# Start offsets of the split weight tiles, and the number of bias buffers, in a two-layer encoder

## The chip, the cores and the metric

The kernel runs on one core of one Trainium2 chip. The core has a matrix engine (TensorE, PE in the rows), which multiplies a stationary operand (the weights, loaded by a separate instruction, PEld) with a moving operand streamed past it; three engines for elementwise work (VectorE or DVE, ScalarE or ACT, GpSimd or POOL); and SyncE (SP), which here only issues DMA transfers, in its own order. [...] The metric is the device time of one execution in microseconds (us).

## The reference, cut to what matters

A trunk of two layers over 256 tokens of width 1024, all in fp32. Each layer is a SwiGLU feed-forward of width 2816, three attention mixers that share one input projection, their gated sum with an output projection, and a second feed-forward.

```python
def swiglu(h, w_in, w_out):
    g, u = jnp.split(h @ w_in, 2, axis=-1)
    return (jax.nn.silu(g) * u) @ w_out

for l in range(DEPTH):                                   # DEPTH = 2
    x = x + 0.5 * swiglu(rmsnorm(x, norm_ffn1[l]), w_ffn1_in[l], w_ffn1_out[l])
    h = rmsnorm(x, norm_mix[l])
    qa, ka, va, qb_, kb, vb, qc, kc, vc, gate_logits = jnp.split(h @ w_in[l], split_points, axis=-1)
    y_a = mixer_a(...)        # dense attention with rotary, 8 heads
    y_b = mixer_b(...)        # windowed attention, 8 heads, with a relative bias
    y_c = mixer_c(...)        # differential attention, 4 heads x 2 maps, with a relative bias
    branches = jnp.einsum('bsnw,nwd->bsnd', jnp.stack([y_a, y_b, y_c], axis=2), w_branch[l])
    merged = jnp.sum(jax.nn.sigmoid(gates) * branches, axis=2)
    x = x + merged @ w_out[l]
    x = x + 0.5 * swiglu(rmsnorm(x, norm_ffn2[l]), w_ffn2_in[l], w_ffn2_out[l])
return rmsnorm(x, norm_final)
```

## The kernel before, in words

**Weights.** All weight matrices together are cut into 196 chunks of 128 x 2048 fp32 (1 MB each), in the order in which they are used (`specs`, lines 261 to 267). `ahead` (line 270) keeps the pipeline full: SP loads chunk after chunk into `raw` tiles (three buffers, line 275), and `split` (line 281) writes each chunk as a sum of two parts: ScalarE rounds it into `hi` (line 291), VectorE computes `lo = raw - hi` (line 292), each in two pieces of 128 x 1024. `whi` and `wlo` have three buffers each. `weights` (line 297) hands chunk i to the matrix code and lets `ahead` run some chunks on.

**Matmuls.** The activations are split in the same way, into `xgh` and `xgl` (or `hh`/`hl`, `yah`/`yal`, `mh`/`ml`). `mm3` (line 303) makes each product of three matmuls: hi x high, hi x low, lo x high. In almost all of them the weights are a 128 x 128 slice of `hi` or `lo` and the activations are the moving operand, 256 columns long. Names of the outputs tell the stage: `gu` is the input side of a feed-forward (88 chunks), `facc` its output side (44 chunks), `fm` a projection in a mixer, `br` a branch projection, `wacc` the mixer's output projection. The two places with 512 columns, where the moving operand is the weight tile and the stationary one an activation slice, are the values `vps` (lines 884 to 886) and the output side of the last feed-forward (lines 390 to 392). TensorE's order is that of the code. A weight load is issued while the matmul ahead of it still runs.

**Where tiles lie.** In the built program's layout `xgh` begins at byte 28224 and `xgl` at 36416, both 64 modulo 512. The `raw`, `hi`, `lo`, `hh`, `hl`, `yah` to `ycl`, `mh` and `ml` tiles all begin at 384 modulo 512. Slices inside the tiles step by 512 or 1024 bytes.

**Bias.** For the 8 heads of mixer B and the 4 of mixer C a tile `G` of 128 x 384 is loaded from the table `skew` in device memory (`bias_tile`, line 573, issued by SP at line 577), up to two steps ahead of its head (`bias_of` in `step`, line 746). `biased` (line 625) reads it twice, on VectorE. `G` has four buffers, so SP waits for the reads of the head four back before it issues the next load. SP issues in order: a weight load that stands behind such a load waits with it. The scheduler of the language places SP's instructions; TensorE's, ScalarE's and VectorE's orders are written by hand where it matters.

Of the kernel before, what the change touches and what calls it, by code (L numbers as in the profile page):

```python
# [11 lines left out]
F32 = mybir.dt.float32  # L12
F32R = mybir.dt.float32r
# [4 lines left out]
P = 128  # L18
# [52 lines left out]
def encoder(ctx: ExitStack, tc: tile.TileContext, a, rope, onehot, out):  # L71
# [3 lines left out]
    whi = ctx.enter_context(tc.tile_pool(name="whi", bufs=3))  # L75
    wlo = ctx.enter_context(tc.tile_pool(name="wlo", bufs=3))
    p1 = ctx.enter_context(tc.tile_pool(name="p1", bufs=2))
# [9 lines left out]
    def f(ap):  # L87
        return ap.bitcast(F32)
# [179 lines left out]
    raws, parts = [], []  # L268

    def ahead(n_raw, n_split):  # L270
        while len(raws) < min(n_raw, len(specs)):
            srcs, shape = specs[len(raws)]
            raw = wraw.tile([P] + shape, F32, tag="raw", name="raw")
            for sl, ap in srcs:
                nc.sync.dma_start(out=raw if sl is None else raw[sl], in_=ap)
            raws.append(raw)
        while len(parts) < min(n_split, len(specs)):
            for _ in split(2):
                pass

    def split(n, eng=None):

        _, shape = specs[len(parts)]
        raw = raws[len(parts)]
        hi = whi.tile([P] + shape, F32R, tag="hi", name="hi")
        lo = wlo.tile([P] + shape, F32R, tag="lo", name="lo")
        parts.append((hi, lo))
        n = shape[0] // n
        for i in range(0, shape[0], n):
            h = slice(i, i + n)  # L290
            nc.scalar.copy(out=hi[:, h], in_=raw[:, h])  # L291
            (eng or nc.vector).tensor_sub(lo[:, h], raw[:, h], f(hi[:, h]))  # L292
            yield
# [278 lines left out]

    def bias_tile(h):

        g = p1.tile([P, 384], F32, name="G", bufs=4)
        src = bass.AP(tensor=skew.tensor, offset=skew.offset + h * P * 512 + 127, ap=[[511, P], [1, 384]])
        nc.sync.dma_start(out=g, in_=src)
        return g
# [24 lines left out]
    def mixer(l):  # L603
# [142 lines left out]
        def bias_of(s):  # L746
            h = s - 8 if s < 16 else B_HEADS + (s - 16) // 2
            if 8 <= s < 24 and ("G", h) not in T:
                T["G", h] = bias_tile(h)
# [192 lines left out]
    with tc.manual_schedule(engines=BY_HAND):  # L942
# [12 lines left out]
        for tt in range(2):  # L955
            for m in range(KT):
                nc.tensor.transpose(xps[m // 2][:, m % 2, cs(tt)], xtok[:, tt, cs(m)], ident)
            warm(4)
        first = split(4, nc.gpsimd)
        for b in range(4):  # L960
            for i in range(2):
# [52 lines left out]
```

## Time and profile before

| what | us |
|---|---|
| median of 2 runs (1221.83 to 1223.14) | 1222.49 |
| the profiled execution | 1221.8 |
| its span, first to last instruction | 1220.0 |
| TensorE busy (97% of the span) | 1188.2 |
| VectorE busy (67%) | 814.7 |
| ScalarE busy (56%) | 677.8 |
| GpSimd busy (23%) | 275.8 |

The span is that of the profiled execution; 1.8 us of its time lie around it. A busy time is the union of an engine's records. Records of matmuls overlap, since each is drawn from its start to the end of its way through the array, so a busy TensorE does not say how densely the matmuls follow each other; the starts in the timeline do. An engine's "idle before" counts only if that engine is waited for.

### The profile page before, as it was taken

What the parts mean: (1) busy time and instruction counts of PE and PEld (TensorE: products, weight loads), DVE (VectorE), ACT (ScalarE), POOL (GpSimd) and SP (SyncE); (2) the same over time, 40 slices, a digit from 0 to 9 for tenths busy, and PEclk for the clock granted to TensorE, in tenths of its full rate; (3) what the DMA queues carried; (4) which work ended last, traced back from release to release, by engine and by line L of the source; (5) the groups of instructions that cost most, each with busy time, mean ns of one, the idle gap of its engine ahead of it and who ended that gap; (6) DMA issues with size and microseconds to landing.
All of it is one profiled execution on the core that took longest, in us unless ns stands there. A gap on an engine that the chain in (4) does not pass through costs nothing.

```text
span 1220.0 us, 23216 instructions
## 1 busy us (share of the span) xinstructions
PE 1188.2 (97%) x9748; PEld 1163.3 (95%) x9748; DVE 814.7 (67%) x1137; ACT 677.8 (56%) x1117; POOL 275.8 (23%) x196
## 2 busy tenths in 40 slices
PE   7999999999999999999999999999999999999997
PEld 6999999899999999999999999999999999999996
DVE  5555557888887675555575555588887967555554
ACT  6444346589876554444453444476998655543433
POOL 2211223300022241212232122232000313212221
PEclk9999999999999999999999999999999999999999
DMA  8568655554545555555555655545443445555550
GB/s 274 192 201 267 224 193 165 167 163 132 176 145 179 173 174 197 184 196 185 185 191 178 202 178 189 191 145 193 148 161 128 163 173 172 197 183 176 190 187 35
DMA packets 169364, 218.15 MB, mean 179 GB/s; under 512 B 4302, under 2 KB 147200, under 8 KB 169260
## 3 DMA queue, kind: packets, MB, share of 16 engines
q1 hardware_dynamic: 168652, 215.09, 53.7%
q8 instruction: 76, 1.25, 0.4%
q10 hardware_dynamic: 464, 1.06, 0.2%
q0 software_dynamic: 144, 0.52, 0.1%
q14 instruction: 28, 0.23, 0.1%
HBM read 215.59 MB, written 4.22 MB: 180 GB/s over the span
## 4 chain that ended last, share of the span: by engine, by line
PE 75%; ACT 11%; DVE 10%; issue 3%; DMA 1%; POOL 1%; POOLq 0%; ACTq 0%; DVEq 0%
PE gu L308 13%; PE gu L309 13%; PE gu L310 13%; PE facc L308 5%; PE facc L310 5%; PE facc L309 5%; DVE lo L292 4%; ACT hi L291 2%; PE fm L308 2%; PE fm L309 2%; PE fm L310 2%; ACT e L601 2%; PE facc L392 2%; PE facc L391 2%; PE facc L390 2%
## 5 line engine op out<-in xcount | busy, mean ns | idle before, releaser
L291 ACT CAST hi<-raw 128x1024 fp32r<-128x1024 f32 (+1 forms) x394 | 399.7, 1044 | 417.0 <-issue 366.2
L292 DVE TENSOR_TENSOR lo<-raw,hi 128x1024 fp32r<-128x1024 f32 x390 | 507.1, 1324 | 139.6 <-ACT hi L291 138.8
L308 PE MATMUL gu<-xgh,hi 128*128 128x256 f32 x1408 | 392.3, 279 | 6.2 <-DVE R L359 5.9
L310 PE MATMUL gu<-xgh,lo 128*128 128x256 f32 x1408 | 391.1, 278 | 1.6 <-POOL lo L292 0.8
L309 PE MATMUL gu<-xgl,hi 128*128 128x256 f32 x1408 | 392.0, 278 | 0.0
L308 PEld LDWEIGHTS gu<-xgh,hi 128*128 128x128 f32 x1408 | 265.1, 188 | 9.1 <-ACT hi L291 6.0
L310 PEld LDWEIGHTS gu<-xgh,lo 128*128 128x128 f32 x1408 | 266.1, 189 | 2.0 <-POOL lo L292 1.1
L309 PEld LDWEIGHTS gu<-xgl,hi 128*128 128x128 f32 x1408 | 265.5, 189 | 1.1
L308 PE MATMUL fm<-xgh,hi 128*128 128x256 f32 x640 | 179.4, 280 | 1.0 <-DVE R L359 1.0
L309 PE MATMUL fm<-xgl,hi 128*128 128x256 f32 x640 | 178.9, 280 | 0.0
L310 PE MATMUL fm<-xgh,lo 128*128 128x256 f32 x640 | 178.2, 278 | 0.0
L483 POOL TENSOR_TENSOR gr<-gr,R 128x512 f32<-128x512 f32 x44 | 84.5, 1921 | 413.6 <-ACT gr L482 413.6
L310 PE MATMUL facc<-hh,lo 128*128 128x256 f32 x528 | 149.2, 283 | 0.0
L308 PE MATMUL facc<-hh,hi 128*128 128x256 f32 x528 | 149.2, 283 | 0.0
L309 PE MATMUL facc<-hl,hi 128*128 128x256 f32 x528 | 149.1, 282 | 0.0
L308 PEld LDWEIGHTS fm<-xgh,hi 128*128 128x128 f32 x640 | 120.6, 188 | 1.9 <-DVE R L359 1.8
L309 PEld LDWEIGHTS fm<-xgl,hi 128*128 128x128 f32 x640 | 120.4, 188 | 0.8 <-DVE xgl L323 0.2
L310 PEld LDWEIGHTS fm<-xgh,lo 128*128 128x128 f32 x640 | 120.7, 189 | 0.0
L310 PEld LDWEIGHTS facc<-hh,lo 128*128 128x128 f32 x528 | 101.0, 191 | 0.0
L309 PEld LDWEIGHTS facc<-hl,hi 128*128 128x128 f32 x528 | 101.0, 191 | 0.0
L308 PEld LDWEIGHTS facc<-hh,hi 128*128 128x128 f32 x528 | 101.0, 191 | 0.0
L488 POOL TENSOR_TENSOR hl<-hid,hh 128x512 fp32r<-128x512 f32 x44 | 76.7, 1744 | 105.7 <-ACT hh L487 102.7
(227 smaller groups left out, 1693.3 us busy)
## 6 DMA issues: line engine op xcount, KB each, us to landing
raw<-in_w_ffn_in_dram SPq DMA_DIRECT2D x87, 1024.0 KB, 5.1
raw<-in_w_ffn_out_dram SPq DMA_DIRECT2D x44, 1024.0 KB, 4.9
raw<-in_w_in_dram SPq DMA_DIRECT2D x38, 1024.0 KB, 5.1
raw<-in_w_branch_dram SPq DMA_DIRECT2D x12, 1024.0 KB, 5.2
raw<-in_w_out_dram SPq DMA_DIRECT2D x8, 1024.0 KB, 5.0
G<-skew SPq DMA_DIRECT2D x24, 192.0 KB, 3.4
raw<-in_w_in_dram SPq DMA_DIRECT2D x8, 512.0 KB, 5.0
skew<-vec_d SPq DMA_DIRECT2D x6, 512.0 KB, 7.5
```

Source lines behind the costliest of these rows:

```text
L291: nc.scalar.copy(out=hi[:, h], in_=raw[:, h])
L292: (eng or nc.vector).tensor_sub(lo[:, h], raw[:, h], f(hi[:, h]))
L308: nc.tensor.matmul(ps, lhsT=hi[:, k, sl], rhs=xh, start=st, stop=False, **chk)
L309: nc.tensor.matmul(ps, lhsT=hi[:, k, sl], rhs=xl, start=False, stop=False, **chk)
L310: nc.tensor.matmul(ps, lhsT=lo[:, k, sl], rhs=xh, start=False, stop=last, **chk)
L390: nc.tensor.matmul(ps, lhsT=xh[:, k, cs(tt)], rhs=w[0][:, k, sl], start=(first and k == 0), stop=False)
L391: nc.tensor.matmul(ps, lhsT=xh[:, k, cs(tt)], rhs=w[1][:, k, sl], start=False, stop=False)
L392: nc.tensor.matmul(ps, lhsT=xl[:, k, cs(tt)], rhs=w[0][:, k, sl], start=False, stop=(last and k == 1))
L483: nc.gpsimd.tensor_mul(gr, gr, Rb)
L488: nc.gpsimd.tensor_sub(hl, hid, f(hh))
L601: nc.scalar.activation(out=e[:, qt, :], in_=e[:, qt, :], func=AF.Identity, scale=su[:, qt:qt + 1])
```

## The change

The tiles `hi` and `lo` are allocated 512 bytes longer per partition (2176 instead of 2048 elements), and the part that is used begins at an offset `off` of 0, 64, ... or 448 bytes. The offset is that of the chunk's number: chunks 0 to 2 begin at 0, chunks 3 to 5 at 64, and so on; chunks 24 to 26 begin at 0 again. `G` gets two buffers instead of four.

```diff
@@ -282,8 +282,9 @@
         _, shape = specs[len(parts)]
         raw = raws[len(parts)]
-        hi = whi.tile([P] + shape, F32R, tag="hi", name="hi")
-        lo = wlo.tile([P] + shape, F32R, tag="lo", name="lo")
+
+        n_el, off = shape[0] * shape[1], 16 * (len(parts) // 3 % 8)
+        hi, lo = (pool.tile([P, n_el + 128], F32R, tag=t, name=t)[:, off:off + n_el].rearrange("p (a b) -> p a b", a=shape[0]) for pool, t in ((whi, "hi"), (wlo, "lo")))
         parts.append((hi, lo))
         n = shape[0] // n
         for i in range(0, shape[0], n):
@@ -572,7 +573,7 @@
     def bias_tile(h):
 
-        g = p1.tile([P, 384], F32, name="G", bufs=4)
+        g = p1.tile([P, 384], F32, name="G", bufs=2)
         src = bass.AP(tensor=skew.tensor, offset=skew.offset + h * P * 512 + 127, ap=[[511, P], [1, 384]])
         nc.sync.dma_start(out=g, in_=src)
         return g
```

The six longer tiles take 3072 bytes more and the two buffers of `G` 3072 less; every other tile stays where it was or moves by 3072 bytes, a multiple of 512. The orders of TensorE, VectorE, ScalarE and GpSimd are the same, row by row, before and after. Only SP's order differs, and in it only which `G` stands in which place. Lines after 285 move by one.

On SP, in the mixer of layer 1, where the loads of `G` stand between weight loads. `G_3263`, `G_3336`, `G_3407`, `G_3474`, `G_3543` and `G_3641` are the tiles of mixer B's heads 2 to 7:

```order
 L275 DMA raw_3370<-in_w_in_dram 128x8x256
-L577 DMA G_3407<-skew_133 128x384
+L578 DMA G_3263<-skew_133 128x384
 L275 DMA raw_3508<-in_w_in_dram 128x8x256
-L577 DMA G_3474<-skew_133 128x384
-L577 DMA G_3543<-skew_133 128x384
-L577 DMA G_3641<-skew_133 128x384
+L578 DMA G_3336<-skew_133 128x384
+L578 DMA G_3407<-skew_133 128x384
+L578 DMA G_3474<-skew_133 128x384
 L275 DMA raw_3608<-in_w_branch_dram 128x4x512
```

The places between the weight loads are the same ones, and each waits for the same head's reads; the tile that is loaded there is that of the head two after the one released, where it was that of the head four after.

On SP, at the end of mixer B in layer 2. `G_11089` is the tile of mixer C's last head, `G_10787` of its second, `G_10946` of its third:

```order
-L577 DMA G_11089<-skew_133 128x384
+L578 DMA G_10787<-skew_133 128x384
 L275 DMA raw_10913<-in_w_branch_dram 128x4x512
 L275 DMA raw_11006<-in_w_in_dram 128x8x256
+L578 DMA G_10946<-skew_133 128x384
+L578 DMA G_11089<-skew_133 128x384
 L275 DMA raw_11123<-in_w_in_dram 128x8x256
 L275 DMA raw_11201<-in_w_in_dram 128x8x256
```

Two loads stand here now that stood further ahead, between two weight loads that had nothing between them; they wait for the reads of mixer C's first and second head.

## Rows read from the trace of the kernel before

**Rows 1.** Page, parts 1 and 2: TensorE and VectorE, busy and by slices, granted clock.
```profile
PE 1188.2 (97%) x9748; PEld 1163.3 (95%) x9748; DVE 814.7 (67%) x1137; ACT 677.8 (56%) x1117; POOL 275.8 (23%) x196
...
PE   7999999999999999999999999999999999999997
...
PEclk9999999999999999999999999999999999999999
```

**Rows 2.** Page, part 4: chain that ended last, share by engine.
```profile
PE 75%; ACT 11%; DVE 10%; issue 3%; DMA 1%; POOL 1%; POOLq 0%; ACTq 0%; DVEq 0%
```

**Rows 3.** Timeline of TensorE: start us, us, engine line, op, out<-in, shape, count.
```profile
694.08 0.29 PE L308 MATMUL gu<-xgh,hi 128*128 128x256 f32 x1
...
704.98 0.28 PE L308 MATMUL facc<-hh,hi 128*128 128x256 f32 x1
...
710.72 0.29 PE L308 MATMUL gu<-xgh,hi 128*128 128x256 f32 x1
```

**Rows 4.** Window: length, busy us of PE, PEld, DVE, ACT, POOL, clock, DMA.
```profile
694.00:699.40 5.40, 5.40 (x49) 5.40 (x49) 2.36 (x2) 2.00 (x2) 0.00 (x0) 1.00 0.72 211
```

**Rows 5.** Timeline of TensorE, mixer of layer 1, a stretch of fm.
```profile
242.03 0.28 PE L309 MATMUL fm<-xgl,hi 128*128 128x256 f32 x1
...
247.45 0.28 PE L310 MATMUL fm<-xgh,lo 128*128 128x256 f32 x1
```

**Rows 6.** Timeline of TensorE, mixer of layer 1, a branch chunk.
```profile
343.91 0.28 PE L308 MATMUL br<-yah,hi 128*128 128x256 f32 x1
...
349.55 0.28 PE L310 MATMUL br<-yah,lo 128*128 128x256 f32 x1
```

**Rows 7.** Timeline of TensorE, mixer of layer 1, values, 512 columns.
```profile
228.66 0.40 PE L884 MATMUL vps<-hi,xgh 128*128 128x512 f32 x1
...
234.85 0.39 PE L884 MATMUL vps<-hi,xgh 128*128 128x512 f32 x1
```

**Rows 8.** Timeline of TensorE, last feed-forward, output side, 512 columns.
```profile
1050.66 0.39 PE L390 MATMUL facc<-hi,hh 128*128 128x512 f32 x1
...
1054.06 0.39 PE L390 MATMUL facc<-hi,hh 128*128 128x512 f32 x1
```

**Rows 9.** Page, part 5: the splits; busy, mean ns, idle before and its releaser.
```profile
L291 ACT CAST hi<-raw 128x1024 fp32r<-128x1024 f32 (+1 forms) x394 | 399.7, 1044 | 417.0 <-issue 366.2
L292 DVE TENSOR_TENSOR lo<-raw,hi 128x1024 fp32r<-128x1024 f32 x390 | 507.1, 1324 | 139.6 <-ACT hi L291 138.8
```

**Rows 10.** Waits: who waited for whom, us in total, times, longest.
```profile
PEld gu L308 <- ACT hi L291: 6.0, 3, 4.7
```

**Rows 11.** Timeline of SP's issues, mixer of layer 1 (x3: from first to last).
```profile
294.45 8.24 SPq L577 DMA_DIRECT2D G<-skew  x3
...
340.98 0.34 SPq L577 DMA_DIRECT2D G<-skew  x1
...
346.85 0.38 SPq L275 DMA_DIRECT2D raw<-in_w_in_dram  x1
```

**Rows 12.** Timeline of VectorE: reads of G, heads 1 (second read), 2 and 3.
```profile
293.93 0.48 DVE L625 CUSTOM_DVE_ANT_0 e<-sc,G,nsink 128x256 f32<-128x256 f32 x1
...
297.18 0.47 DVE L625 CUSTOM_DVE_ANT_0 e<-sc,G,nsink 128x256 f32<-128x256 f32 x1
...
301.46 0.47 DVE L625 CUSTOM_DVE_ANT_0 e<-sc,G,nsink 128x256 f32<-128x256 f32 x1
```

**Rows 13.** The tile G: its loads, ns min/median/max to issue; us to landing.
```profile
L577 SPq DMA_DIRECT2D G<-skew x24: 319/338/737, 118.1 to 918.7; - x24
...
DMA to landing us min/median/max: 2.3/3.4/4.8
```

**Rows 14.** Timeline of SP's issues, mixer of layer 2, two weight loads.
```profile
929.13 0.38 SPq L275 DMA_DIRECT2D raw<-in_w_in_dram  x1
...
943.11 0.37 SPq L275 DMA_DIRECT2D raw<-in_w_in_dram  x1
```

**Rows 15.** Line 292: its instructions, ns min/median/max, first and last start.
```profile
L292 DVE TENSOR_TENSOR lo<-raw,hi x390: 1149/1224/2320, 15.8 to 1198.1; 128x1024 fp32r<-128x1024 f32 x195
```

## The prediction

> **What bounds the kernel now.** I read the page first. TensorE is busy for 1188.2 of 1220.0 us, the next engine is VectorE with 67%, and the granted clock stands at full speed, the 2.4 GHz level, in every slice [rows 1]. The chain that ended last is TensorE for 75%; ScalarE and VectorE hold 21%, in the mixers and at stage edges [rows 2]. So what counts is how fast matmuls follow each other, and the busy column does not tell that, because the records of neighbours overlap. I therefore read start times from TensorE's timeline and divide by the number of starts.
>
> In one feed-forward step of layer 2, 96 `gu` matmuls start between 694.08 and 704.98 us, which is 113.5 ns each, and the 48 `facc` matmuls after them take until 710.72 us, which is 119.6 ns each [rows 3]. Both move 256 columns at the same clock (a window over the `gu` part shows 1.00 [rows 4]), and neither has an idle gap. 256 columns at 2.4 GHz are 106.7 ns, so either kind loses something, 6.8 and 12.9 ns. What differs is where the operands lie. While matmul n streams its moving operand, the weights of matmul n+1 are loaded. In the built program's layout `hi`, `lo`, `hh`, `hl` and the tiles that `branch` and `w_out` move begin at 384 bytes modulo 512, and `xgh`, `xgl` at 64; all slices step by 512 or 1024. I call next weights minus current moving operand, modulo 512, the distance: 320 for `gu` and `fm`, 0 for `facc`, `wacc` and `br`.
>
> Over all 256-column matmuls that follow without a pause, the starts give 114.4 ns for 4157 of `gu`, 115.6 for 1841 of `fm`, and 119.6 to 120.0 for `facc`, `br` and `wacc`. Weighted, that is 114.8 ns at distance 320 and 119.7 ns at distance 0. Not every piece at 320 runs alike: 47 starts of `fm` from 242.03 to 247.45 us lie 117.8 ns apart [rows 5]. That the loop's shape is the reason speaks less well: `br` accumulates into one bank as `fm` does, yet its 48 starts from 343.91 to 349.55 us are 120.0 ns apart [rows 6].
>
> One more distance can be read, at 512 columns. The value matmuls `vps` have distance 192 and start every 229.3 ns (27 gaps, 228.66 to 234.85 us) [rows 7]; the last stage's `facc` has distance 0 and starts every 226.7 ns (15 gaps, 1050.66 to 1054.06 us) [rows 8]. So 192 is no better than 0, but worse by 2.6 ns.
>
> **The change, part by part.** *Offsets.* `hi` and `lo` of chunk c begin (c // 3 % 8) times 64 bytes later, so each of eight distances gets about an eighth of the 196 chunks, for all stages. No instruction is added and the orders on TensorE, VectorE, ScalarE and GpSimd stay as they are. What changes is the gap of 8688 matmuls of 256 columns: 6144 of `gu` and `fm` (now 114.8 ns) and 2544 of `facc`, `br` and `wacc` (now 119.7 ns). For the eight distances I take: 0 at 119.7 (read); 320 at 114.8 (read); 192 at 121.0, since a 512-column matmul moves twice as much and I carry half of its 2.6 ns over; and five that no row shows (64, 128, 256, 384, 448). Those are bounded below by 106.7 ns, the columns over the clock, and above by 122.3, which is 119.7 plus all of the 2.6. I take 117.2, midway between the two read at 256 columns, because three read distances spread to both sides of it. The mean of eight is (119.7 + 114.8 + 121.0 + 5 x 117.2) / 8 = 117.7 ns.
>
> Then `gu` and `fm` lose 6144 x 2.9 = 17.8 us, and the other stages win 2544 x 2.0 = 5.1 us: a loss of 12.7 us. The 96 `vps` and 264 `facc` matmuls of 512 columns can move by about 2.6 ns each either way, 0.9 us in all; I count nothing. TensorE is busy in nine tenths of nearly every slice, so I count the loss whole; by its 75% of the chain alone it would be 9.5 us.
>
> *The splits.* ScalarE and VectorE write `hi` and `lo` at the new starts, with the same shapes: 1044 ns and 1324 ns each [rows 9]. No row shows them at another start. I take no change; below, nothing is won, since neither is the bound; above, VectorE has a third of the span idle, and TensorE's weight loads waited for `hi` 6.0 us in all [rows 10]. Were that cover gone, every ns more on 390 VectorE splits would cost 0.39 us.
>
> *Two bias buffers.* 24 loads of `G` remain. A load now waits for the head two before it, not four; SP's slots, behind which the weight loads queue, stay at the same releases, as the order shows. What is late next is the head that reads it. The tightest in layer 1: head 1 ends its last read at 294.41 us, SP issues at 294.45, and head 3 begins its first at 301.46 [rows 11, 12]. Landing took 2.3 to 4.8 us [rows 13], so 2.2 us are left at worst. Two issues are new in layer 2, behind the weight load at 929.13 us; the next weight load went out only at 943.11 us [rows 14], and in layer 1 the loads in these slots were out by 341.32 us, with the weight load behind them at 346.85 [rows 11]. Cost: nothing, covered by heads that are 4 us and more apart; were one landing late by 2 us in each of 24 heads, at most some 48 us, which the row above speaks against.
>
> The sum, against the profiled execution: 1220.0 us of span and 1.8 us around it are 1221.8, 0.7 below the median shown. 1221.8 + 12.7 gives 1234.5; I say **1234 us**.
>
> A rule of the Trainium skill speaks against this whole sum. TensorE: Matmul & The Clock Gate, section Part 2 (step by step), says the weight load and the moving operand have two independent read ports, so loading the next weights takes no bandwidth from the running matmul. By it the distance would not matter and the time would stay; 119.6 beside 113.5 ns in one step [rows 3] speaks against it here. The same page, section on the 56 ns gap, has N over 2.4 GHz plus some 2.5 ns for back-to-back bf16 matmuls, 109 ns for 256 columns by my estimate; no stage here reaches it.
>
> **The rivals.** *Only distance 0 is bad, the other seven are as 320.* For it: 320 was not chosen and is mild. Against it: 192 is as bad as 0 at 512 columns. Mean (119.7 + 7 x 114.8) / 8 = 115.4; `gu` and `fm` lose 3.7, the others win 10.9: 1215 us.
>
> *Slower: 320 is the one good distance.* For it: two of the three distances read are at 119.7 or more, and 71% of these matmuls stand at 320 today and would leave it. With the other seven at 120.5 the mean is 119.8: 30.7 us for `gu` and `fm`, 0.3 for the rest: 1253 us. It becomes more than 2% (24.4 us) once the mean passes 119.05, that is, once the five unseen average over 119.4.
>
> *Faster: the unseen distances lose nothing or little.* If they lie as far below 320 as that lies below 0, at 109.9, the mean is 113.1 and the time 1195 us; at the bound of 106.7 it is 1177. For it: 6.8 ns above the columns are still lost at 320. Against it: no 256-column row is below 113. It passes 2% when the five average under 110.3.
>
> *The change doesn't do what it says.* The gap goes with the stage (its operands, its banks), not with the distance: 1222 us. For it: within this trace each stage has one distance, so the two are not parted. Against it: `br` and `fm`.
>
> **How the numbers follow.** Mixed distances, as summed, 1225 to 1246 us: 0.40. Only 0 bad: 0.18. Stage, not distance: 0.08. 320 alone good: 0.24. Unseen ones free: 0.10. A measurement of this kernel can tell about 2% from no change, so the first three are within 2% (0.66), the fourth is slower (0.24), the fifth faster (0.10). The range leaves out the faster case and the end of the slower one: 1208 to 1256 us.
>
> **What would show it.** In the changed kernel's timeline the `gu` and `facc` gaps should step every three chunks, through the same values at the same distance in both stages; a `facc` piece at 320 should read about 114 and a `gu` piece at 0 about 120 ns. If both keep their values, it was the stage. `G` reads should begin when they did, as counted from the end of the head before, and VectorE's splits should keep 1224 ns as their usual value [rows 15]. Wrong would be: gaps under 113 or over 122 ns at several distances, a new idle time of TensorE, or a wait of line 625's reads for a DMA.

## The result, and the profile of the changed kernel

The changed kernel takes 1236.24 us (median of 2 runs, 1234.98 to 1237.50) beside 1222.49 us before: a ratio of 1.011, 95% interval 1.0088 to 1.0132. It is slower by 13.75 us, which is within the 2% called the same. The prediction was 1234 us. The profiled execution's span grew from 1220.0 to 1233.2 us.

The page of the changed kernel, lines that answer to [rows 1, 2, 9] (in this kernel the split stands in lines 292 and 293, the matmul helper in 309 to 311):

```profile
PE 1203.4 (98%) x9748; PEld 1178.1 (96%) x9748; DVE 814.4 (66%) x1137; ACT 677.4 (55%) x1117; POOL 275.6 (22%) x196
...
PE 76%; DVE 10%; ACT 8%; issue 2%; POOL 1%; DMA 1%; POOLq 0%; ACTq 0%; DVEq 0%
...
L292 ACT CAST hi<-raw 128x1024 fp32r<-128x1024 f32 (+1 forms) x394 | 399.1, 1042 | 430.9 <-issue 373.9
L293 DVE TENSOR_TENSOR lo<-raw,hi 128x1024 fp32r<-128x1024 f32 x390 | 506.7, 1323 | 136.3 <-ACT hi L292 135.5
```

TensorE's busy time grew by 15.2 us, and that of VectorE, ScalarE and GpSimd moved by at most 0.4 us. A split costs 1042 and 1323 ns beside 1044 and 1324 ns before: where it writes makes no difference to it. The answer for the tile `G` ends with

```profile
DMA to landing us min/median/max: 2.3/3.3/4.9
```

against 2.3/3.4/4.8 [rows 13], and it lists no idle time of VectorE ahead of the reads of `G`.

Where the time went is shown by windows over the stages. Each goes from the first `gu` or `fm` matmul of a stage to that of the next; columns as in [rows 4]. Of the kernel before, first the three feed-forward stretches (layer 1's first; its second with layer 2's first; the last), then the two mixers:

```profile
8.70:202.50 193.80, 187.58 (x1591) 185.57 (x1591) 114.44 (x125) 90.70 (x118) 47.27 (x30) 0.99 0.66 218
428.90:799.70 370.80, 369.77 (x3183) 368.40 (x3182) 220.14 (x217) 168.69 (x210) 94.77 (x61) 1.00 0.57 188
1025.20:1212.00 186.80, 186.28 (x1343) 175.24 (x1342) 105.30 (x105) 81.60 (x106) 44.99 (x28) 1.00 0.49 164
...
202.50:428.90 226.40, 218.59 (x1798) 213.76 (x1797) 185.08 (x340) 165.92 (x339) 42.86 (x36) 1.00 0.50 160
799.70:1025.20 225.50, 218.55 (x1799) 213.88 (x1798) 185.31 (x336) 165.41 (x337) 43.67 (x37) 1.00 0.49 159
```

The same of the changed kernel:

```profile
8.60:206.10 197.50, 190.85 (x1591) 188.81 (x1590) 114.44 (x124) 90.54 (x117) 47.17 (x30) 0.99 0.65 212
432.30:810.80 378.50, 377.47 (x3183) 376.17 (x3182) 220.18 (x218) 168.34 (x211) 94.79 (x61) 1.00 0.56 184
1036.00:1224.30 188.30, 187.78 (x1343) 175.93 (x1343) 104.91 (x106) 81.81 (x107) 44.77 (x28) 1.00 0.49 163
...
206.10:432.30 226.20, 220.04 (x1798) 215.42 (x1798) 185.13 (x339) 165.97 (x338) 42.90 (x36) 1.00 0.49 160
810.80:1036.00 225.20, 219.88 (x1798) 215.42 (x1798) 185.43 (x337) 165.37 (x338) 43.68 (x37) 1.00 0.49 161
```

The feed-forward stretches grew from 751.4 to 764.3 us, by 12.9; the mixers went from 451.9 to 451.4. The loss stands in the feed-forwards; the mixers, where `fm` runs, got 0.5 us shorter. The granted clock (the column behind the five busy times, 0.99 to 1.00) is the 2.4 GHz level in both.

How the pieces run shows TensorE's timeline of the changed kernel in layer 2's feed-forward, first start of each `gu` piece (96 matmuls) and `facc` piece (48), the place of [rows 3]:

```profile
680.71 0.28 PE L309 MATMUL facc<-hh,hi 128*128 128x256 f32 x1
...
686.46 0.29 PE L309 MATMUL gu<-xgh,hi 128*128 128x256 f32 x1
...
697.36 0.28 PE L309 MATMUL facc<-hh,hi 128*128 128x256 f32 x1
...
703.01 0.29 PE L309 MATMUL gu<-xgh,hi 128*128 128x256 f32 x1
...
714.54 0.28 PE L309 MATMUL facc<-hh,hi 128*128 128x256 f32 x1
...
737.20 0.28 PE L309 MATMUL gu<-xgh,hi 128*128 128x256 f32 x1
...
748.71 0.28 PE L309 MATMUL facc<-hh,hi 128*128 128x256 f32 x1
...
754.46 0.29 PE L309 MATMUL gu<-xgh,hi 128*128 128x256 f32 x1
```

Addresses and distances are counted in bytes within one partition, one of the 128 rows of a tile. By the addresses in the built program the first four pieces and the last two have the distances 256, 64, 320, 128 and 256, 0. Differences over counts give 119.8, 113.5, 117.7, 120.1 and 119.9, 119.8 ns. So a `gu` piece now runs at 113.5, 120.1 or 119.9 ns, where it ran at 113.5 ns in this stretch before. Over all 256-column matmuls that follow without a pause, and for the 512-column ones apart:

| distance, bytes modulo 512 | 0 | 64 | 128 | 192 | 256 | 320 | 384 | 448 |
|---|---|---|---|---|---|---|---|---|
| 256 columns, ns (812 to 1306 gaps each) | 119.8 | 115.6 | 118.9 | 117.6 | 119.8 | 115.7 | 119.0 | 117.6 |
| `gu` alone | 119.9 | 114.1 | 119.3 | 117.8 | 119.9 | 114.4 | 119.0 | 117.8 |
| `facc` alone | 119.8 | 117.8 | 118.6 | 116.9 | 119.8 | 117.7 | 118.7 | 116.7 |
| `facc` of the last stage, 512 columns | 227.3 | 233.4 | 232.4 | 229.6 | 227.3 | 233.4 | 232.4 | 229.5 |

Distances 256 apart read alike in every row, within 0.4 ns. The mean of the eight is 118.0 ns.

These are means over pieces that run at different steady gaps. At 64 and 320, 11 of the 26 pieces with 36 or more gaps settle at 113.3 or 113.4 ns and 15 at 117.8. At 192 and 448 22 of 24 settle at the same 117.8 ns, and two at 113.3. One of these two is a `facc` piece at 192:

```profile
74.82 0.28 PE L309 MATMUL facc<-hh,hi 128*128 128x256 f32 x1
...
80.27 0.28 PE L309 MATMUL gu<-xgh,hi 128*128 128x256 f32 x1
```

(80.27 - 74.82) / 48 is 113.5 ns with the first gap of 120. So the 2 ns by which 192 stands behind 64 in the table come from how often a piece is fast, and not from another gap of its own. A kernel that holds 192 everywhere was not run.

### The profile page after: what moved, and what is told of

It is laid out like the page before. It is cut to its first block, busy times and chain, and to the rows that moved or that the text cites. A ratio compares the mean times of both kernels' runs of the same rounds, so it can differ in the third digit from the quotient of the medians.

```text
span 1233.2 us, 23226 instructions
## 1 busy us (share of the span) xinstructions
PE 1203.4 (98%) x9748; PEld 1178.1 (96%) x9748; DVE 814.4 (66%) x1137; ACT 677.4 (55%) x1117; POOL 275.6 (22%) x196
## 4 chain that ended last, share of the span: by engine, by line
PE 76%; DVE 10%; ACT 8%; issue 2%; POOL 1%; DMA 1%; POOLq 0%; ACTq 0%; DVEq 0%
PE gu L309 13%; PE gu L310 13%; PE gu L311 13%; PE facc L310 5%; PE facc L309 5%; PE facc L311 5%; DVE lo L293 4%; PE fm L309 3%; PE fm L310 3%; PE fm L311 3%; ACT hi L292 2%; PE facc L392 2%; PE facc L393 2%; PE facc L391 2%; PE wacc L310 1%
## 5 line engine op out<-in xcount | busy, mean ns | idle before, releaser
L292 ACT CAST hi<-raw 128x1024 fp32r<-128x1024 f32 (+1 forms) x394 | 399.1, 1042 | 430.9 <-issue 373.9
L293 DVE TENSOR_TENSOR lo<-raw,hi 128x1024 fp32r<-128x1024 f32 x390 | 506.7, 1323 | 136.3 <-ACT hi L292 135.5
L309 PE MATMUL gu<-xgh,hi 128*128 128x256 f32 x1408 | 396.6, 282 | 6.6 <-DVE R L360 6.3
L311 PE MATMUL gu<-xgh,lo 128*128 128x256 f32 x1408 | 395.8, 281 | 1.6 <-POOL lo L293 0.8
L310 PE MATMUL gu<-xgl,hi 128*128 128x256 f32 x1408 | 396.4, 282 | 0.0
```

Of the source, the lines that this page charges most:

```text
L309: nc.tensor.matmul(ps, lhsT=hi[:, k, sl], rhs=xh, start=st, stop=False, **chk)
L310: nc.tensor.matmul(ps, lhsT=hi[:, k, sl], rhs=xl, start=False, stop=False, **chk)
L311: nc.tensor.matmul(ps, lhsT=lo[:, k, sl], rhs=xh, start=False, stop=last, **chk)
```

## The experiments

All have two buffers of `G`, so that the first one says what that half of the change costs. Lines of the helper move by some numbers between kernels. Each kernel's ratio is to runs of the kernel before on the same chip.

**Two bias buffers alone.**

```
-        g = p1.tile([P, 384], F32, name="G", bufs=4)
+        g = p1.tile([P, 384], F32, name="G", bufs=2)
```

> The kernel before with two G buffers instead of four and no offsets. Theory (the loss comes from the distance between weights and moving operand alone): same time as before, 1222 us, ratio 1.000 within 0.002, gaps 114.8 and 119.7 ns as before. Rival (the later loads of G cost something, a wait of line 625's reads for a DMA): up to all of the 13.7 us of the change, ratio 1.011.

1224.71 us beside 1223.71: a ratio of 1.0011 (1.0002 to 1.0021). The gaps stay at 114.8 ns (`gu`, `fm`) and 119.75 ns (the rest), and the answer for `G` lists no idle time of VectorE ahead of its reads. The two buffers cost at most 0.2%, and where the 1.0 us comes from is not shown; the other 1% is the offsets'. The offsets with four buffers of `G` were not run.

**The moving operand shifted, the weights left alone.** `xgh` and `xgl` move by 320 bytes, so that `gu` and `fm` come to distance 0; no weight part moves.

```
+    pad0 = const.tile([P, 80], F32, name="pad0")
+    nc.vector.memset(pad0, 0.0)
     xgh = const.tile([P, KT, S], F32R, name="xgh")
     xgl = const.tile([P, KT, S], F32R, name="xgl")
+    pad1 = const.tile([P, 48], F32, name="pad1")
+    nc.vector.memset(pad1, 0.0)
```

> Weights without offsets, two G buffers; xgh and xgl are moved by 320 bytes, from 64 to 384 modulo 512, so that gu and fm stand at distance 0 without a byte of the weights moved. Theory (the distance decides, whichever side moves): gu and fm go from 114.8 to 119.8 ns as facc has, 6144 x 5.0 = +30.7 us, about 1253 us, ratio 1.025; facc, br, wacc unchanged. Rival 1 (the stage's loop decides, not the distance): 1222 us. Rival 2 (the start of the weight tile decides, not its distance to the moving operand): 1222 us.

1245.76 us, a ratio of 1.0186 (1.0172 to 1.0200). Its TensorE timeline, the same place, a `gu` piece and the `facc` piece behind it:

```profile
692.99 0.28 PE L312 MATMUL gu<-xgh,hi 128*128 128x256 f32 x1
...
704.51 0.28 PE L312 MATMUL facc<-hh,hi 128*128 128x256 f32 x1
...
710.27 0.28 PE L312 MATMUL gu<-xgh,hi 128*128 128x256 f32 x1
```

(704.51 - 692.99) / 96 is 120.0 ns where it was 113.5, and `facc` is at 120.0 as before. Two small memsets at the start and the two buffers of `G` apart, nothing about the stage, its banks, its weights or its instructions changed, only where the moving operand begins. So the distance is the cause and not the stage. The rule weighed in the prediction (the Trainium skill, TensorE: Matmul & The Clock Gate, Part 2 (step by step)) says that the two operands have independent read ports, so that the weight load takes no bandwidth from the running matmul. By it the gap would stay, and these rows do not agree: 120.0 beside 113.5 ns. What the matmuls wait for is not shown.

The time came out some 7 us below the 1253 us that the theory had. `fm` did rise, from 115.6 to 119.9 ns, which over 1920 matmuls is 8.1 us, but the mixers did not get longer by it. Its first mixer, by the window:

```profile
209.10:435.70 226.60, 221.93 (x1798) 217.91 (x1798) 185.59 (x340) 165.85 (x338) 42.83 (x36) 1.00 0.49 160
```

226.60 us beside 226.40 before, with TensorE busy 3.3 us longer: its idle time went from 7.8 to 4.7 us. A slower `fm` is paid out of TensorE's waiting.

**Only `facc`, `br` and `wacc` shifted, by 64 bytes.** `gu` and `fm` stay at 320, the others go from 0 to 64. `stagger` holds the chunks whose weights these three stages use.

```
-        hi = whi.tile([P] + shape, F32R, tag="hi", name="hi")
-        lo = wlo.tile([P] + shape, F32R, tag="lo", name="lo")
+        n_el, off = shape[0] * shape[1], 16 if len(parts) in stagger else 0
+        hi, lo = (pool.tile([P, n_el + 128], F32R, tag=t, name=t)[:, off:off + n_el].rearrange("p (a b) -> p a b", a=shape[0]) for pool, t in ((whi, "hi"), (wlo, "lo")))
```

> Longer tiles and two G buffers as in the change, but a fixed offset by stage: 0 for gu, fm, the values and the last output side, 64 bytes for the chunks of facc (first three feed-forwards), br and wacc, whose distance becomes 64. Theory (the gap is a function of the distance with a period of 256 bytes): gu and fm stay at 114.8, the others go from 119.7 to the 117.5 or so that the changed kernel shows for them at 64 and 320, 2544 x 2.2 = 5.6 us won, about 1217 us, ratio 0.9955. Rival (a mix of offsets is what the changed kernel's gaps rest on, a fixed one gives others): no gain, 1222 us, or the 114 ns of gu at the same distance also here, 14 us won, 1208 us.

1220.72 us, a ratio of 0.9974 (0.9965 to 0.9983): a gain of 3.0 us where 5.6 were expected, although the gaps fell as forecast (`facc` to 117.7 ns, the three stages to 117.0). In its profiled execution the stages are together 3.9 us shorter and the first `gu` matmul starts 1.9 us later; why is not shown. The rival's 114 ns at the same distance did not come for `facc`. The timeline:

```profile
693.54 0.29 PE L317 MATMUL gu<-xgh,hi 128*128 128x256 f32 x1
...
704.44 0.28 PE L317 MATMUL facc<-hh,hi 128*128 128x256 f32 x1
...
710.09 0.29 PE L317 MATMUL gu<-xgh,hi 128*128 128x256 f32 x1
```

`gu` 113.5 ns, `facc` 117.7 ns. Gap by gap, `gu` has 113, 113, 114, 113, ..., and `facc` after its first two 117, 118, 118, 117, ... to its end, in all 30 pieces that were read. So at a good distance there are two steady paces, 113.3 and 117.8 ns, and a piece keeps the one it entered. The `fm` piece at 117.8 ns in [rows 5] has the second of them.

**Finer offsets, 0 to 112 bytes in steps of 16.**

```
-        n_el, off = shape[0] * shape[1], 16 * (len(parts) // 3 % 8)
+        n_el, off = shape[0] * shape[1], 4 * (len(parts) // 3 % 8)
```

(The line taken away is that of the changed kernel.)

> The change with steps of 16 bytes instead of 64: offsets 0, 16, ... 112, another one every three chunks; gu and fm see the distances 320 to 432, the others 0 to 112. Theory A (the gap follows lines of 64 bytes, a shift inside one does nothing): gu reads 114.3 at 320 to 368 and 119.1 at 384 to 432, about 117 on average; the others 119.8 at 0 to 48 and 117.7 at 64 to 112; about 1234 us. Theory B (it follows the byte distance smoothly): values between those in even steps, nearly the same time, 1235 us. Theory C (finer structure, for example 16 or 32 bytes): some distance gives less than 113 ns or more than 122 ns.

1239.41 us, a ratio of 1.0131 (1.0113 to 1.0150). 64 and 320 are at 115.3 and 115.1 ns; the other fourteen distances read, 16 to 48, 80 to 112 and 336 to 432 among them, lie between 118.0 and 119.9. At 16 bytes beside 64 (48 and 80) the gap is 118.9 and 118.8 ns.

**Offsets 0, 4, 8, 12 and 240 to 252 bytes.**

```
-        n_el, off = shape[0] * shape[1], 16 * (len(parts) // 3 % 8)
+        n_el, off = shape[0] * shape[1], (0, 1, 2, 3, 60, 61, 62, 63)[len(parts) // 3 % 8]
```

> The change with offsets of 0, 4, 8, 12, 240, 244, 248, 252 bytes: gu and fm see 320 to 332 and 48 to 60, the others 0 to 12 and 240 to 252. Theory A (only multiples of 16 bytes count, within 16 nothing changes): 320 to 332 all as 320 (114.4), 48 to 60 all as 48 (118.9). Theory B (the fast lock is a narrow well around 64 and 320): values rise by single words on both sides, up to about 118.8 at 16 bytes. Theory C (the well's bottom lies beside 64): some distance within 16 bytes reads below 113. In all of them about 1236 us.

1235.38 us in one run. By distance modulo 256, ns:

| 0 | 4 | 8 | 12 | 48 | 52 | 56 | 60 | 64 | 68 | 72 | 76 | 240 | 244 | 248 | 252 |
|---|---|---|---|---|---|---|---|---|---|---|---|---|---|---|---|
| 119.6 | 118.3 | 115.8 | 116.9 | 118.8 | 114.2 | 117.8 | 119.5 | 115.4 | 118.4 | 118.3 | 113.8 | 119.6 | 119.8 | 117.8 | 119.9 |

52 and 76, 12 bytes to either side of 64, are better than 64 here: all 16 of their pieces with 36 or more gaps settle at 113.3 ns, where at 64 seven of ten do and three at 117.8. 4 and 8 bytes aside are not good. A kernel that holds 52 or 76 everywhere was not run. This is neither a narrow well round 64 nor a matter of multiples of 16, and no rule for these values was found. Which of them would be good elsewhere has to be read, not derived.

**`lo` 192 bytes behind `hi`.** Within a triple of matmuls the distances then alternate: 320, 0, 320 for `gu`, 0, 192, 0 for `facc`.

```
+        n_el = shape[0] * shape[1]
+        hi, lo = (pool.tile([P, n_el + 128], F32R, tag=t, name=t)[:, off:off + n_el].rearrange("p (a b) -> p a b", a=shape[0]) for pool, t, off in ((whi, "hi", 0), (wlo, "lo", 48)))
```

> All hi tiles at offset 0, all lo tiles at offset 192 bytes, two G buffers. In each triple of gu and fm the first matmul (own weights hi, next hi) keeps distance 320 either way; the second (own hi, next lo) has 320 to its own weights and 0 to the next; the third (own lo, next hi) has 0 to its own and 320 to the next. Theory (the load of the NEXT weights meets the running stream): the gap after the second matmul is the long one of the triple. Rival (a matmul's own weights decide): the gap after the third is. In both, gu lies between 114 and 120 ns on average, facc (0, 0, 192) near 119, about 1232 us.

1234.88 us in one run. It does not tell what it was made for: no gap of the triple stands out (118.0, 117.7 and 117.6 ns in `gu`, 118.8, 117.8 and 116.9 in `facc`). A mean of two gaps of 113.3 and one of 120 would be 115.5; all stages read 117.8. Matmuls of mixed distances do not each take the time of their own, and whether a matmul's next or its own weights count stays open here (the kernels with other borders, below, bear on it).

**Every distance 64, borders between stages too** (called e9 further on). `xgh` and `xgl` at 384 bytes as above, all weights 64 bytes into their tiles.

```
+        n_el, off = shape[0] * shape[1], 16
+        hi, lo = (pool.tile([P, n_el + 128], F32R, tag=t, name=t)[:, off:off + n_el].rearrange("p (a b) -> p a b", a=shape[0]) for pool, t in ((whi, "hi"), (wlo, "lo")))
```

> xgh and xgl at 384 modulo 512 as the other moving tiles, all weights 64 bytes later: every 256-column matmul, stage borders included, has distance 64. Theory (at 64 a stretch locks at 113.3 or at 117.8 ns, by the gaps at its entry: after gaps of 121 and 122 ns at distance 0 it runs at 113.3, without them at 117.8): no border at distance 0 is left, so gu and facc run at 117.8: the feed-forwards gain 4224 x 3.4 - 1584 x 1.9, +11 us, about 1234 us. Rival (borders with other distances are what throws a stage into the slow mode): all run at 113.3, -14 us in the feed-forwards, about 1208 us. Either way the mixers hardly change.

1210.00 us (1208.27 to 1210.82), a ratio of 0.9886 (0.9869 to 0.9903): faster than the kernel before, clear of the noise though within the 2% called the same. Its timeline and its chain:

```profile
681.05 0.28 PE L312 MATMUL facc<-hh,hi 128*128 128x256 f32 x1
...
686.49 0.28 PE L312 MATMUL gu<-xgh,hi 128*128 128x256 f32 x1
...
697.37 0.28 PE L312 MATMUL facc<-hh,hi 128*128 128x256 f32 x1
...
PE 68%; ACT 13%; DVE 13%; issue 4%; DMA 1%; POOL 1%; POOLq 0%; ACTq 0%; DVEq 0%
```

(686.49 - 681.05) / 48 and (697.37 - 686.49) / 96 are both 113.3 ns. All 1583 `facc` gaps are 113 or 114, and the mean of `gu` is 113.6. The forecast of 1234 us (a uniform 64 would run at the slow pace) fell: the slow pace of `facc` in the kernel that shifts only the rest is not the distance's own.

In the profiled executions the feed-forward stretches are 10.8 us shorter than before (740.6 for 751.4) and the two mixers 2.8 us (449.1 for 451.9). In a mixer the gain stands at its end, where 192 `wacc` matmuls follow each other without idle time. Their first start and that of the `gu` behind them, in layer 1 of the kernel before and then of this one:

```profile
405.90 0.28 PE L308 MATMUL wacc<-mh,hi 128*128 128x256 f32 x1
...
428.94 0.29 PE L308 MATMUL gu<-xgh,hi 128*128 128x256 f32 x1
...
403.78 0.28 PE L312 MATMUL wacc<-mh,hi 128*128 128x256 f32 x1
...
425.54 0.28 PE L312 MATMUL gu<-xgh,hi 128*128 128x256 f32 x1
```

That is 23.04 and 21.76 us. So a mixer pays for the gap of `wacc`, where it did not for that of `fm` when the moving operand was shifted.

**The same distance in all stages, other borders** (e10). `xgh` and `xgl` at 448, `gu` and `fm` weights 128 bytes into their tiles, `facc`, `br` and `wacc` 64. Inside each stage the distance is 64 again; from `gu` to `facc` it is 0, back it is 128.

```
+        n_el, off = shape[0] * shape[1], 16 if len(parts) in stagger else (32 if shape != [2, D] else 0)
```

> xgh and xgl at 448 modulo 512, weights of gu and fm at offset 128, of facc, br and wacc at 64, of the last output side at 0: all stages have distance 64, the border from gu to facc has 0, that from facc to gu 128. Theory (a border at distance 0 throws the stage after it into the fast lock): facc runs at 113.3 instead of 119.7, 1320 x 6.3 = 8.3 us won; gu now enters after 128 and may run at 113.3 (1214 us in all) or at 117.8 (+14 us for gu, 1228 us). Rival (the border does not matter): facc at 117.8 as in the kernel with a fixed offset by stage, gu at 114.4: about 1219 us.

1224.38 us, a ratio of 1.0006 (0.9995 to 1.0016): none of the numbers expected. The timeline:

```profile
680.42 0.28 PE L321 MATMUL gu<-xgh,hi 128*128 128x256 f32 x1
...
691.73 0.29 PE L321 MATMUL facc<-hh,hi 128*128 128x256 f32 x1
...
697.19 0.28 PE L321 MATMUL gu<-xgh,hi 128*128 128x256 f32 x1
```

`gu` 117.8 ns, `facc` 113.8 with its entry: the reverse of the kernel with only `facc` shifted. Over the crossings between `gu` and `facc` without a pause, the distance of the one matmul at the border and the pace ahead of it together go with the pace of all that follow. A border at 0 changes the pace, one at 128 or 384 leaves it slow, one at 64 keeps it:

| crossing, distance of its one matmul | pace ahead | pace behind |
|---|---|---|
| `gu` to `facc`, 0 | 117.8 | 113.3 in 26 of 26 |
| `gu` to `facc`, 0 | 113.3 | 117.8 in 4 of 4 |
| `facc` to `gu`, 128 | 113.3 | 117.8 in 23 of 23 |
| `facc` to `gu`, 128 | 117.8 | 117.8 in 4 of 4 |
| with only `facc` shifted: `gu` to `facc`, 384 | 113.3 | 117.8 in 29 of 29 |
| with only `facc` shifted: `facc` to `gu`, 0 | 117.8 | 113.3 in 27 of 27 |
| all 64: either way, 64 | 113.3 | 113.3 in 57 of 57 |

The borders from `wacc` to `gu`, two in each kernel, fit this but for one: at 128 behind the slow pace one went slow and one fast.

Here a matmul's distance to its own weights is 64 in every stage, as in e9, and the pace still changes at the borders. So its own weights alone do not decide. Whether it is the next weights against the running operand, or the step from one moving operand to the next, is not parted.

**Borders at 320 instead of 64, and the last stage at 0.** Two kernels to part the border from the operand's own address. The first has `xgh` and `xgl` at 128 bytes and the `gu` weights 320 into their tiles: 64 inside the stages, 320 at the borders. The second is the kernel with 64 everywhere, but for the 512-column weights of the last output stage, at distance 0.

```
-        n_el, off = shape[0] * shape[1], 16 if len(parts) in stagger else (32 if shape != [2, D] else 0)
+        n_el, off = shape[0] * shape[1], 16 if len(parts) in stagger else (80 if shape != [2, D] else 0)
...
+        n_el, off = shape[0] * shape[1], 16 if len(parts) in stagger else (16 if shape != [2, D] else 0)
```

> xgh and xgl at 128 bytes modulo 512 (e9 had 384, e10 448); weights of gu and fm begin 320 bytes into their tiles, those of facc, br and wacc 64, of the last output 0. Inside every stage the distance is 64, as in e9 and e10; at the border gu to facc and back it is 320, which is 64 modulo 256 (e10 had 0 and 128 there, e9 64). Theory that the border sets at which of two paces a stretch at 64 runs, and that distances count modulo 256: every gu and facc piece at 113.3 ns, 1210 us, as e9. Rival, that the moving operand's own address decides (e9's 384 was good, e10's 448 not): 128 is 64 past a multiple of 256 no better than 448, so gu mixed or at 117.8 ns, 1224 us. Rival, that any change of address at a border breaks the pace: 1220 to 1228 us.

> e9 (distance 64 everywhere) with one edit: the weights of the last output stage, whose 256 matmuls move 512 columns, begin 0 bytes into their tiles, so their distance is 0, not 448. In e9 these ran at 229.0 ns, in the kernel before at 227.3. Theory, that the distance decides there too: 226.7 to 227.3 ns and 0.5 us less than e9, about 1209.5 us. Rival, that the new border to the last stage or the stage's other waits decide: e9's 1210.0 us or more. Either way it repeats e9's feed-forwards, which should be at 113.3 ns again.

1212.52 us (1210.89 to 1217.72; ratio 0.9912, 0.9895 to 0.9928) and 1214.23 us (1212.18 to 1216.25; ratio 0.9930, 0.9912 to 0.9948). A border at 320 keeps the pace as one at 64 does: fast stays fast from `gu` to `facc` in 26 of 26 and back in 24 of 24, slow stays slow in 7 of 7; the second kernel, with 64 at these borders, has the same counts. So distances count modulo 256 at the border as well, and the operand's own address is not the reason. But both kernels run a part of layer 1's first feed-forward at the slow pace, the second one from 32 to 97 us, so that its feed-forwards do not repeat e9's as expected. Its timeline, where it changes:

```profile
80.28 0.28 PE L321 MATMUL gu<-xgh,hi 128*128 128x256 f32 x1
...
91.59 0.28 PE L321 MATMUL facc<-hh,hi 128*128 128x256 f32 x1
...
97.13 0.28 PE L323 MATMUL facc<-hh,lo 128*128 128x256 f32 x1
97.34 0.25 PE L179 MATMUL ps_g<-ident,rows 38*128 38x38 f32 x1
97.52 1.02 PE L199 MATMUL ps_v<-oneh,relb 32*12 32x511 f32 x2
98.47 0.38 PE L321 MATMUL gu<-xgh,hi 128*128 128x256 f32 x1
...
109.48 0.28 PE L321 MATMUL facc<-hh,hi 128*128 128x256 f32 x1
...
114.92 0.28 PE L321 MATMUL gu<-xgh,hi 128*128 128x256 f32 x1
```

`gu` from 80.28 runs at 117.8 ns; after three small matmuls of other shapes the next pieces run at 113.3 ns, (114.92 - 109.48) / 48. With one distance throughout, nothing at the borders changes the pace any more, so what an entry after an interruption gave lasts until the next interruption. What at an entry sets the pace was not found.

In the last stage the 512-column gap fell from 228.9 to 227.8 ns as the theory of distance had it, 0.3 us for 264 matmuls. More was lost beside it. In the last feed-forward nine `gu` pieces of 96 matmuls follow a piece of 512 columns. All nine now settle at 117.8 ns, in both kernels; in e9, with the 512-column weights 64 bytes into their tiles (distance 448), all nine settle at 113.3. One such piece, first start and that of the `facc` behind it, of e9 and then of the second kernel:

```profile
1111.28 0.28 PE L312 MATMUL gu<-xgh,hi 128*128 128x256 f32 x1
...
1122.18 0.39 PE L394 MATMUL facc<-hi,hh 128*128 128x512 f32 x1
...
1114.05 0.28 PE L321 MATMUL gu<-xgh,hi 128*128 128x256 f32 x1
...
1125.35 0.40 PE L403 MATMUL facc<-hi,hh 128*128 128x512 f32 x1
```

That is 10.90 and 11.30 us. An estimate from these rows is 9 x 0.4 = 3.6 us for the last feed-forward and some 550 x 4.5 ns = 2.5 us for the slow part of the first, less the 0.3 us won and 0.8 us for fewer gaps of 213 ns (14 against 22 near 30 us, the 1.2 GHz level): 5.0 us, where the second kernel's profiled execution (1212.85 us) stands 4.6 above e9's (1208.27). So the edit's own 0.3 us is outweighed by the pace behind it. The first kernel's profiled execution is its slowest, 1217.72 us; it also ran longer at the 1.2 GHz level (granted clock 0.50 from 28.4 to 33.6 us). The other runs have no trace, so why they differ by 4 to 7 us is not shown.

## Why the prediction was right, point by point

- **TensorE's gaps bound the kernel:** right for the feed-forwards, whose 12.9 us make up the loss, and for `wacc` at the end of a mixer. Wrong for `fm`, which is most of a mixer's share.
- **The distance, not the stage, sets the gap:** right. Shifting the moving operand alone took `gu` from 113.5 to 120.0 ns. The rival of the stage falls, and with it the 1222 us.
- **The eight distances:** 0 was 119.8 as read. 320 was 115.7 where 114.8 was carried over from `gu` and `fm`; the sentence that a `facc` piece at 320 would read about 114 was wrong (117.7), since a piece at a good distance may run at the slow pace. 192 was taken as 121.0 and is 117.6: carrying half of the 2.6 ns from 512 columns [rows 7, 8] to 256 was a wrong step. The table shows that best and worst change places between the two: 64 and 320 are the best at 256 columns and the worst at 512, where the weight tile is the moving operand. The five unseen averaged 118.2, where 117.2 was taken. The two errors nearly cancel: 118.0 beside 117.7 ns.
- **The sum:** `gu` and `fm` rose by 3.06 ns (2.9 predicted), the others fell by 1.5 (2.0 predicted). Counted whole that is 18.8 - 3.8 = 15.0 us. But of the mixers' share of it, 4.8 us for `fm` less 1.6 for `br` and `wacc`, the loss did not show: the mixers got 0.5 us shorter. What shows is `gu`, 4224 x 3.32 = 14.0, `facc` 1584 x -1.40 = -2.2, and `facc` at 512 columns, 264 x 3.6 = 1.0: 12.8 beside 12.9 us measured. Counting the loss whole because TensorE is busy in nine tenths of a slice was a wrong step; `busy` is no sign that a stage is bound there, and the ScalarE and VectorE share in [rows 2], which the prediction itself put in the mixers, was the place to look. The 512-column matmuls, put at nothing, cost their upper bound of about 0.9 us.
- **The splits:** nothing, as forecast (1042 and 1323 ns).
- **Two bias buffers:** forecast nothing; alone they cost 1.0 us or 0.1% (1.0002 to 1.0021), which is not nothing but small; no read of `G` waits in that trace, so the 2.2 us left at worst were enough.
- **The rivals:** only 0 bad falls, since 128, 256 and 384 are at 119 to 120. 320 alone good is nearly it, since 64 and 320 have the lowest means of the eight; but 192 and 448 lie between, with the same two paces, the mean is 118.0, and the point from which it would have been more than 2%, 119.05, was not reached. The unseen ones free falls: no mean is below 113.

The forecast was thus right in mechanism and sign for the feed-forwards. That it came within 3 us is in part luck: against the 12.7 us forecast the gaps were worth 15.0, 3.2 of these did not show in the mixers, and the 512-column matmuls put at nothing added 1.0.

## What to carry to other kernels

With 256-column matmuls back to back, where the next weights begin against the current moving operand, modulo 256 bytes, was worth 6% here (113.3 against 120.0 ns). In a kernel that lets its pools set this address, read the gaps by stage, and hold the good distance everywhere, borders included, instead of spreading it. Then read piece by piece which of the two paces each stage entered, since the same distance ran at both. Spreading over all distances gives their mean, which is a loss wherever most of the work stood at a good one. Before a gap is multiplied by a count, look at whether TensorE waits for other engines in that stage, as it does around `fm`: there a slower matmul was paid out of the waiting.

## What the runs showed of the hardware that was not expected

- Two steady paces at the same distance and the granted clock of 1.00: gaps of 113, 113, 114 (113.3 ns) or 117, 118, 118 (117.8 ns), kept for 30 us and more, changed by one matmul at another distance or by an interruption. 192 and 448 have the same two.
- Best and worst distance change places at 512 columns: 227.3 ns at 0 and 256, 233.4 at 64 and 320; 192 stays ahead of 128 in both (229.6 and 232.4 ns).
- 12 bytes beside 64 modulo 256 are good (114.2 and 113.8 ns, every long piece at 113.3), 4, 8 and 16 bytes beside it are not (117.8 to 119.5). This is one run.
- With 64 in all other stages, the 256-column pieces behind a 512-column piece at distance 0 ran at the slow pace in 9 of 9 (two kernels), behind one at 448 in none of 9.
